# A decoder trunk on one core: the feed-forward input's sums, splits and products in another order

## The chip, the cores and the metric

One Trainium2 chip, of which the kernel uses one core. The time is the device time of one execution in microseconds (us). Three runs of the kernel before took 1914.89, 1920.9 and 1922.11 us, so its median is 1920.9 us. One further execution was taken with the hardware profiler; all durations below come from that one.

## The reference

Two layers; each is a feed-forward block, a mixing block and another feed-forward block. All matrices are float32, the sequence has 512 positions, the width is 1024, and the inner width of the feed-forward is 2816. The change is inside the feed-forward:

```python
def swiglu(x, w_in, w_out):
    gate, up = jnp.split(x @ w_in, 2, axis=-1)
    return (jax.nn.silu(gate) * up) @ w_out

for l in range(DEPTH):
    hn = rms_norm(h, g_ffn1[l]) * (1.0 + sc1) + sh1
    h = h + 0.5 * (1.0 + gt1) * swiglu(hn, w_ffn1_in[l], w_ffn1_out[l])
    ...   # the mixing block
    hn = rms_norm(h, g_ffn2[l]) * (1.0 + sc3) + sh3
    h = h + 0.5 * (1.0 + gt3) * swiglu(hn, w_ffn2_in[l], w_ffn2_out[l])
```

So a feed-forward takes the normed rows `hn`, multiplies them by a gate matrix and an up matrix, and sends silu(gate) times up through an output matrix. Four such blocks run one after the other.

## The kernel before, in words

**Precision.** TensorE multiplies in a shortened float32, so every operand is split in two: ScalarE (ACT) casts it to a high half, and VectorE (DVE) subtracts to get the low half. In the profile these are the line 101 CAST (`wH`, `comH`) and the line 102 TENSOR_TENSOR (`wL`, `comL`). One product then takes three matmuls: high by high, high by low, low by high. Split weights live in four buffers for `wH` and four for `wL`, which rotate.

**The input of a feed-forward.** The 22 blocks of 128 inner columns are 11 pairs, in two groups (pairs 0 to 5 and 6 to 10); after each group its part of the output matrix is multiplied. The first pairs of a block (four in the very first feed-forward, two in the three others) are multiplied directly, in `projector` (line 98). All later pairs, 34 over the whole kernel, go through `pair_in`, which saves one of eight sub-products by a scheme of sums: seven products of 24 matmuls (line 441 to 443) instead of eight. For the gate and up weights a11, a12, a21, a22 of one pair and the halves B of `hn`, it needs combined rows of `hn` (`P1`, `P2`, `T3`, `T4`, made once per feed-forward by `whole` and `combine`) and combined weights:

1. `S` = row sum of a21 and a22, times P1, into bank `ps_f`; ACT copies the result out (`up`, line 459);
2. the first product, a11 times B11, into bank `ps_d`; ACT copies it out (`s1`, line 463);
3. the last product (a22 times T4) of the *pair before*, which was left waiting (`flush`); the first pair of a group has nothing waiting here;
4. the second weight sum, `S` plus a11 (line 464), times P2, added on top of `ps_d`; ACT copies it out (`s2`, line 468);
5. the corner product, a12 times B21, into bank `ps_g`; DVE adds `s1` (`gate`, line 472) and ACT applies silu;
6. the third sum times T3, added on top of `ps_d`;
7. the sum `S` plus a12 (line 474), times B22, into `ps_f`.

Products 2, 4 and 6 share one bank: each may start only when the copy of what was there before has been read out.

**What sets the order.** A list scheduler writes out one fixed order for each engine from the order of the program text, its own cost estimates and the free buffers. On the chip every engine works through its own list strictly in order and waits at an instruction until what it needs is there. The loads of the weights are issued from SP's queue, the adding loads (which sum two weight blocks while loading) from POOL's queue, each in order too. `issue_after(x)` makes what is written inside it stand behind instruction x on x's own engine.

Of the kernel before, what the change touches and what calls it, by code (L numbers as in the profile page):

```python
# [11 lines left out]
AF = mybir.ActivationFunctionType  # L12
ALU = mybir.AluOpType
# [44 lines left out]
def trunk_kernel(ctx, tc, ins, out, layers=L, phases=("ffn1", "mix", "ffn2")):  # L58
    nc = tc.nc
# [11 lines left out]
    tt, stt, ts = nc.vector.tensor_tensor, nc.vector.scalar_tensor_tensor, nc.vector.tensor_scalar  # L71
    act, mm = nc.scalar.activation, nc.tensor.matmul

    def E(name="e", dt=F32):
        return sp.tile([P, T], dt, name=name, tag="e", bufs=4)
# [4 lines left out]
    def psum(shape, name, tag="x"):  # L80
        return ps.tile(shape, F32, name=name, tag=tag, bufs=2)
# [18 lines left out]
    def split(hi, lo, src):  # L100
        nc.scalar.copy(hi, src)  # L101
        nc.vector.tensor_sub(lo, src, hi.bitcast(F32))  # L102
# [261 lines left out]
    def ffn(l, w_in, w_pair, w_out, hn, im, ss, need, then, ready, first=None):  # L364
# [6 lines left out]
        with tc.tile_pool(name="act", bufs=1) as ap_:  # L371
            com = {n: tuple(ap_.tile([P, 4, H2], F32R, name=x, tag="com", bufs=8) for x in ("comH", "comL")) for n in ("P1", "P2", "T3", "T4")}
            ap_.tile([P, (512 - GAP) // 4], F32, name="gap", tag="gap")
            n_first = 2 if first is None else 4
            tiles = (t for t in projector([w_in[l, j, g] for j in range(2 * n_first) for g in range(2)], hn, BANKS[:3], first, 1, ready) if t is not None)
            xs, waiting, done, after = {}, [], [None], [None]

            def flush():
                for f in waiting:
                    done[0] = f()  # L380
                waiting.clear()

            def hl(w):
                pair = tuple(wp.tile([P, KD, P], F32R, name=x, tag=x, bufs=4) for x in ("wH", "wL"))
                split(*pair, w)
                return pair

            def raw(src, tag=None):
                w = (ap_.tile if tag else wp.tile)([P, KD, P], F32, name=tag or "wraw", tag=tag or "wraw", bufs=1 if tag else 2)
                with tc.issue_after(after[0].ins) if after[0] else nullcontext():  # L390
                    nc.sync.dma_start(w, src)
                return w

            def plus(w, src):
                nc.gpsimd.dma_start(w, src, accum_op=ALU.add)

            def new_x(p):

                X = tuple(ap_.tile([P, 2, T], F32R, name=x, tag="act", bufs=12) for x in ("actH", "actL"))
                for i in range(2):  # L400
                    xs[2 * p + i] = tuple(x[:, i] for x in X)
                return X
# [30 lines left out]
            P1, P2, T3, T4 = ([tuple(t[:, k] for t in com[n]) for k in range(4)] for n in ("P1", "P2", "T3", "T4"))  # L433
            B11, B21, B22 = ([tuple(t[:, sl] for t in hn[k0 + k]) for k in range(4)] for k0, sl in ((0, lo_), (4, lo_), (4, hi_)))

            def prod(pt, w, x, start):

                for i in range(2):
                    for k in range(4):
                        wH, wL = (t[:, 4 * i + k] for t in w)  # L440
                        mm(pt[:, i], wH, x[k][0], start=start and i + k == 0, stop=False, skip_group_check=True)  # L441
                        mm(pt[:, i], wH, x[k][1], start=False, stop=False, skip_group_check=True)  # L442
                        mm(pt[:, i], wL, x[k][0], start=False, stop=k == 3, skip_group_check=True)  # L443

            def put(X, sl, x):
                nc.scalar.copy(X[0][:, :, sl], x)
                return tt(X[1][:, :, sl], x, X[0][:, :, sl].bitcast(F32), ALU.subtract)

            def pair_in(p):
                A = lambda g, kh: w_pair[l, p, g, kh]  # L450
                turns = ("r0", "r1") if p % 2 else ("r1", "r0")
                pD, pF, pG = (psum([P, 2, H2], n, t) for n, t in zip(("ps_d", "ps_f", "ps_g"), ("mm",) + turns))
                X = new_x(p)
                half_ = lambda n: E(n).rearrange("p (i t) -> p i t", i=2)
                S = raw(A(1, 0), ("sum0", "sum1")[p % 2])
                plus(S, A(1, 1))
                prod(pF, hl(S), P1, True)
                up = half_("up")
                nc.scalar.copy(up, pF)
                a11 = raw(A(0, 0), "first")  # L460
                prod(pD, hl(a11), B11, True)
                s1 = half_("s1")
                nc.scalar.copy(s1, pD)  # L463
                tt(S, S, a11, ALU.add)
                flush()
                prod(pD, hl(S), P2, False)
                s2 = half_("s2")
                nc.scalar.copy(s2, pD)  # L468
                a12 = raw(A(0, 1))
                prod(pG, hl(a12), B21, True)  # L470
                gate = half_("gate")
                tt(gate, pG, s1, ALU.add)
                act(gate, gate, AF.Silu)
                tt(S, S, a12, ALU.add)
                S3 = raw(A(0, 0), "third")
                plus(S3, A(1, 0))
                prod(pD, hl(S3), T3, False)
                tt(up, pD, up, ALU.add)
                prod(pF, hl(S), B22, False)
                tt(s2, pF, s2, ALU.add)  # L480
                act(s2, s2, AF.Silu)
                tt(up, s2, up, ALU.mult)
                put(X, hi_, up)

                def rest():
                    prod(pD, hl(raw(A(1, 1))), T4, False)
                    tt(gate, pD, gate, ALU.mult)
                    return put(X, lo_, gate)

                waiting.append(rest)  # L490
# [8 lines left out]
                    yield k0, n, load_w(w_out[l, i, :, k0 : k0 + n], n, w)  # L499


            when = {8 * (n_first == 4) + m: n for m, n in ((1, 0), (3, 1), (4, "P1"), (5, "P2"), (6, "T3"), (7, "T4"))}
            beside = lambda m: m in when and (combine if type(when[m]) is str else whole)(when[m])
            crep = ada_crep(ap_) if n_first == 4 else None
            for g, (j0, j1) in enumerate(GROUPS):
                for p in range(j0 // 2, j1 // 2):
                    if p < n_first:
                        X = new_x(p)
                        for j in (2 * p, 2 * p + 1):
                            pg = next(tiles)  # L510
                            beside(2 * j)
                            pu = next(tiles)
                            s = E("silu")
                            act(s, pg, AF.Silu)
                            stt(s, s, -1.0, pu, ALU.mult, ALU.mult)
                            nc.scalar.copy(xs[j][0], s)
                            behind = tt(xs[j][1], s, xs[j][0].bitcast(F32), ALU.subtract)
                            beside(2 * j + 1)
                            if n_first == 4:
                                ada_steps(ap_, crep, (0, 0, 4, 4, 0, 3, 0, 0)[j], behind)  # L520
                    else:
                        after[0] = None if g or p > n_first + 1 else loads[-2]
                        pair_in(p)
                        after[0] = None
# [26 lines left out]
            n = (j1 - j0) // 2  # L551
# [693 lines left out]
    for n, (l, p) in enumerate(seq):  # L1245
        im = what[p][1]
        nss = new_ss() if n + 1 < len(seq) else None
        nxt, ws = [], []

        def then():  # L1250
            if nss is None:
                return [lambda *_: None] * 5
            nhn, scale, *steps = normed(n + 1, nss)
            nxt.append(nhn)
            scale()
            l2, p2 = seq[n + 1]
            if p2 == "mix":
                srcs = [ins["wmi"][l2, k] for k in range(4)]
            else:
                srcs = [ins["w1i" if p2 == "ffn1" else "w2i"][l2, *divmod(k, 2)] for k in range(4)]  # L1260
            return steps + [lambda k, raw: ws.append(load_w(srcs[k], KD, raw))]

        if p == "mix":
            with tc.tile_pool(name="mix", bufs=1) as mp:
                marks = mix(l, hn, nss, mp, then, ready)
        else:
            w, need = ("w1", (l, 7)) if p == "ffn1" else ("w2", (l + 1, 1))
            marks = ffn(l, ins[w + "i"], ins[w + "p"], ins[w + "o"], hn, im, nss, need, then, ready, first)
        first = None
        hn, ready = (nxt[0], (ws, marks)) if nxt else (None, None)  # L1270
# [85 lines left out]
```

## Time and profile before

| what | value |
|---|---|
| median of three runs | 1920.9 us |
| the profiled execution's own time | 1922.28 us |
| its span, first to last instruction | 1920.5 us |
| TensorE (PE) busy | 1884.7 us, 98% |
| DVE busy | 1400.5 us, 73% |
| ACT busy | 838.1 us, 44% |
| `pair_in` calls | 34, of which 8 are the first of a group |
| matmuls of one pair | 7 x 24 = 168 |

The rows of the timeline read: start in us, length in us, engine, line, operation, output<-input, shapes, count, and in brackets the idle time of that engine just before, with what ended it. A matmul's length in the rows (0.28 us) is modelled and overlaps the next one; from start to start two matmuls of 256 columns are 0.11 us apart. PEld is the load of a matmul's weights. In a view of windows, each row is one stretch of time with the busy time and number of matmuls in it and the granted clock of TensorE (1.00 is full).

### The profile page before, as it was taken

To read this page: it belongs to the slowest core of one execution; us is meant where nothing else is said; L and a number is where in the kernel's file an instruction comes from. 1 tells how busy PE (TensorE), PEld (TensorE's weight loads), DVE (VectorE), ACT (ScalarE), POOL (GpSimd) and SP (SyncE) were. 2 spreads that over 40 slices of the span, in tenths; PEclk is the share of its full clock that TensorE was granted. 3 is DMA by queue.
4 is the path that set the end of the run, shared out by engine and by line. 5 is a ranking of instruction groups with operands and counts; after the bars stand their busy time and mean duration, and the time that the engine had idled before them with its cause. 6 is when DMAs were issued, how large, how long until landed. Compare 5 with 4: busy or idle time off the path is not lost. (4 is left out here: it accounts for less than half of the span.)

```text
span 1920.5 us, 37038 instructions
## 1 busy us (share of the span) xinstructions
PE 1884.7 (98%) x15504; PEld 1747.4 (91%) x15504; DVE 1400.5 (73%) x2181; ACT 838.1 (44%) x1264; POOL 130.9 (7%) x212
## 2 busy tenths in 40 slices
PE   8999999999999999999999999999999999999999
PEld 7998899997889999899899989989878899988998
DVE  7687687758976777777867777876598677773862
ACT  4443355356322554155345514544552234532551
POOL 0101100000000001100100020010000000110000
PEclk9999999999999999999999999999999999999999
DMA  7767877421322476877726688781212306765741
GB/s 299 250 165 227 264 194 237 156 69 46 79 60 62 122 198 178 296 201 197 258 73 182 169 264 236 199 278 41 88 54 50 98 23 184 183 212 136 197 139 59
DMA packets 104326, 308.46 MB, mean 161 GB/s; under 512 B 23392, under 2 KB 24416, under 8 KB 103136
## 3 DMA queue, kind: packets, MB, share of 16 engines
q1 hardware_dynamic: 75936, 203.33, 32.2%
q0 software_dynamic: 28224, 102.77, 21.4%
q8 instruction: 121, 1.98, 0.4%
q14 instruction: 45, 0.37, 0.1%
HBM read 302.66 MB, written 3.41 MB: 159 GB/s over the span
## 5 line engine op out<-in xcount | busy, mean ns | idle before, releaser
L101 ACT CAST wH<-wraw 128x1024 fp32r<-128x1024 f32 (+2 forms) x292 | 268.3, 922 | 511.7 <-PE ps_mm L91 175.2
L102 DVE TENSOR_TENSOR wL<-wraw,wH 128x1024 fp32r<-128x1024 f32 (+2 forms) x292 | 308.2, 1059 | 106.7 <-ACT wH L101 105.1
L90 PE MATMUL ps_mm<-actH,wH 128*128 128x512 f32 (+1 forms) x784 | 288.5, 368 | 0.0
L91 PE MATMUL ps_mm<-actL,wH 128*128 128x512 f32 (+1 forms) x784 | 288.0, 367 | 0.0
L92 PE MATMUL ps_mm<-actH,wL 128*128 128x512 f32 (+1 forms) x784 | 288.0, 367 | 0.0
L441 PE MATMUL ps_d<-comH,wH 128*128 128x256 f32 x816 | 228.9, 280 | 4.4 <-ACT s L463 3.6
L443 PE MATMUL ps_d<-comH,wL 128*128 128x256 f32 x816 | 227.3, 279 | 0.0
L442 PE MATMUL ps_d<-comL,wH 128*128 128x256 f32 x816 | 227.3, 279 | 0.0
L98 PE MATMUL ps_mm<-hnH,wH 128*128 128x256 f32 x1040 | 213.6, 286 | 5.8 <-ACT hnH L101 2.9
L98 PE MATMUL ps_mm<-hnL,wH 128*128 128x256 f32 x1040 | 211.8, 283 | 0.0
L98 PE MATMUL ps_mm<-hnH,wL 128*128 128x256 f32 x1040 | 209.3, 281 | 0.5 <-DVE wL L102 0.5
L163 DVE SCALAR_TENSOR_TENSOR wada<-wada,crep 128x1024 f32<-128x1024 f32 x140 | 167.9, 1220 | 46.3 <-DMA wada<-in_wadaT 46.0
L102 DVE TENSOR_TENSOR wL<-sum,wH 128x1024 fp32r<-128x1024 f32 x102 | 124.9, 1225 | 75.8 <-ACT wH L101 75.6
L98 PEld LDWEIGHTS ps_mm<-hnH,wH 128*128 128x128 f32 x1040 | 159.3, 189 | 16.7 <-issue 8.2
L101 ACT CAST wH<-sum 128x1024 fp32r<-128x1024 f32 x102 | 107.5, 1054 | 152.0 <-PE ps_d L442 71.4
L92 PEld LDWEIGHTS ps_mm<-actH,wL 128*128 128x128 f32 x784 | 147.8, 188 | 24.4
L90 PEld LDWEIGHTS ps_mm<-actH,wH 128*128 128x128 f32 x784 | 147.8, 189 | 24.2
L91 PEld LDWEIGHTS ps_mm<-actL,wH 128*128 128x128 f32 x784 | 147.8, 189 | 24.2
L98 PEld LDWEIGHTS ps_mm<-hnL,wH 128*128 128x128 f32 x1040 | 160.0, 189 | 6.7 <-issue 5.7
L98 PEld LDWEIGHTS ps_mm<-hnH,wL 128*128 128x128 f32 x1040 | 159.8, 190 | 4.0 <-issue 2.9
L441 PEld LDWEIGHTS ps_d<-comH,wH 128*128 128x128 f32 x816 | 155.2, 190 | 6.9 <-ACT s L463 5.1
L442 PEld LDWEIGHTS ps_d<-comL,wH 128*128 128x128 f32 x816 | 155.3, 190 | 0.0
(402 smaller groups left out, 4245.5 us busy)
## 6 DMA issues: line engine op xcount, KB each, us to landing
wada<-in_wadaT POOLq DMA_DIRECT2D x128, 512.0 KB, 4.9
wraw<-in_wmi SPq DMA_DIRECT2D x40, 512.0 KB
wraw<-in_w2p SPq DMA_DIRECT2D x36, 512.0 KB
wraw<-in_w1p SPq DMA_DIRECT2D x32, 512.0 KB
wraw<-in_w1o SPq DMA_DIRECT2D x32, 384.0 KB
wraw<-in_w2o SPq DMA_DIRECT2D x32, 384.0 KB
wraw<-in_w1i SPq DMA_DIRECT2D x20, 512.0 KB
wraw<-in_w1o SPq DMA_DIRECT2D x32, 320.0 KB
```

The source lines that it names most:

```text
L90: mm(acc, wH, xH, start=start, stop=False)
L91: mm(acc, wH, xL, start=False, stop=False)
L92: mm(acc, wL, xH, start=False, stop=stop)
L98: mm(acc[:, sl], w[a][:, k], x[b][:, sl], start=start and n == 0 and sl is HALVES[0], stop=stop and n == 2, skip_group_check=True)
L101: nc.scalar.copy(hi, src)
L102: nc.vector.tensor_sub(lo, src, hi.bitcast(F32))
L163: stt(w, w, 1.0, crep, ALU.mult, ALU.mult, accum_out=out_)
L441: mm(pt[:, i], wH, x[k][0], start=start and i + k == 0, stop=False, skip_group_check=True)
L442: mm(pt[:, i], wH, x[k][1], start=False, stop=False, skip_group_check=True)
L443: mm(pt[:, i], wL, x[k][0], start=False, stop=k == 3, skip_group_check=True)
```

## The change

```diff
--- before
+++ after
@@ pair_in @@
                 a11 = raw(A(0, 0), "first")
                 prod(pD, hl(a11), B11, True)
                 s1 = half_("s1")
-                nc.scalar.copy(s1, pD)
+                copied = nc.scalar.copy(s1, pD)
                 tt(S, S, a11, ALU.add)
+
+                def corner():
+                    a12 = raw(A(0, 1))
+                    prod(pG, hl(a12), B21, True)
+                    gate = half_("gate")
+                    tt(gate, pG, s1, ALU.add)
+                    act(gate, gate, AF.Silu)
+                    return a12, gate
+
+                early = None if waiting else corner()
                 flush()
-                prod(pD, hl(S), P2, False)
+                with tc.issue_after(copied.ins):
+                    second = hl(S)
+                prod(pD, second, P2, False)
                 s2 = half_("s2")
                 nc.scalar.copy(s2, pD)
-                a12 = raw(A(0, 1))
-                prod(pG, hl(a12), B21, True)
-                gate = half_("gate")
-                tt(gate, pG, s1, ALU.add)
-                act(gate, gate, AF.Silu)
+                a12, gate = early or corner()
                 tt(S, S, a12, ALU.add)
                 S3 = raw(A(0, 0), "third")
                 plus(S3, A(1, 0))
@@ ffn @@
-            when = {8 * (n_first == 4) + m: n for m, n in ((1, 0), (3, 1), (4, "P1"), (5, "P2"), (6, "T3"), (7, "T4"))}
+            turns_ = (9, 11, 12, 13, 14, 15) if n_first == 4 else (0, 1, 2, 3, 4, 5)
+            when = dict(zip(turns_, (0, 1, "P1", "P2", "T3", "T4")))
             beside = lambda m: m in when and (combine if type(when[m]) is str else whole)(when[m])
```

Three edits. The cast of the second weight sum to its high half stands behind the copy of the first product on ACT, in all 34 pairs. In the first pair of a group the corner product is written before the second one, so in the place that the waiting product of the pair before has in other pairs. In the three feed-forwards with two direct pairs the row sums and combined rows are written at places 0 to 5 of the direct pairs instead of 1, 3, 4, 5, 6, 7; the first feed-forward keeps its places. Nothing is added to the computation or taken from it.

What the scheduler makes of it shows at three places. First ACT in the first `pair_in` of the second feed-forward. Names: `sum_7803` is S of that pair and `sum_8003` that of the next, `wraw` is a12, `third` the third sum; the first row with `sum_7803` splits S plus a11, the second one S plus a12; `s_7866` is s1, and s2 is `s_7897` before and `s_7930` in the change. Before:

```order
L101 CAST wH<-sum_7803 128x1024
L101 CAST wH<-wraw 128x1024
L516 CAST actH<-silu 128x512
L101 CAST wH<-third 128x1024
L459 COPY up<-ps_f 128x512
L101 CAST wH<-sum_7803 128x1024
L463 COPY s_7866<-ps_d 128x512
L101 CAST wH<-sum_8003 128x1024
L468 COPY s_7897<-ps_d 128x512
```

and in the change (lines behind 463 are 8 or more higher):

```order
L101 CAST wH<-wraw 128x1024
L523 ACTIVATE silu<-ps_mm 128x512
L525 CAST actH<-silu 128x512
L459 COPY up<-ps_f 128x512
L463 COPY s_7866<-ps_d 128x512
L101 CAST wH<-sum_7803 128x1024
L101 CAST wH<-third 128x1024
L471 ACTIVATE gate<-gate 128x512
L101 CAST wH<-sum_7803 128x1024
L480 COPY s_7930<-ps_d 128x512
```

Before, the cast of S plus a12 stood ahead of the copy s1; now both casts of S stand behind s1, and the cast of S plus a12 stands ahead of the copy s2. On DVE, same pair, before:

```order
L464 TENSOR_TENSOR sum_7803<-sum_7803,first 128x1024
L515 SCALAR_TENSOR_TENSOR silu<-silu,ps_mm 128x512
L102 TENSOR_TENSOR wL<-sum_7803,wH 128x1024
L102 TENSOR_TENSOR wL<-wraw,wH 128x1024
L517 TENSOR_TENSOR actL<-silu,actH 128x512
L474 TENSOR_TENSOR sum_7803<-sum_7803,wraw 128x1024
L102 TENSOR_TENSOR wL<-third,wH 128x1024
```

and in the change:

```order
L464 TENSOR_TENSOR sum_7803<-sum_7803,first 128x1024
L102 TENSOR_TENSOR wL<-wraw,wH 128x1024
L524 SCALAR_TENSOR_TENSOR silu<-silu,ps_mm 128x512
L526 TENSOR_TENSOR actL<-silu,actH 128x512
L102 TENSOR_TENSOR wL<-sum_7803,wH 128x1024
L102 TENSOR_TENSOR wL<-third,wH 128x1024
L470 TENSOR_TENSOR gate<-ps_g,s_7866 128x512
L482 TENSOR_TENSOR sum_7803<-sum_7803,wraw 128x1024
L102 TENSOR_TENSOR wL<-sum_7803,wH 128x1024
```

The split of a12 moved up, right behind S plus a11; S plus a12 moved down, behind the split of the third sum and the addition of the corner product.

The second place is PE in the same pair, from the end of the second product (`ps_d<-comH`) to the third; waits are shown. Before, the rest of the corner product stood there:

```order
L443 MATMUL ps_d<-comH,wL 128x256
L442 MATMUL ps_g<-hnL,wH 128x256
L443 MATMUL ps_g<-hnH,wL 128x256
...
L441 MATMUL ps_f<-hnH,wH 128x256
L442 MATMUL ps_f<-hnL,wH 128x256
L441 MATMUL ps_d<-comH,wH 128x256 [waits Activation_49]
```

and in the change:

```order
L443 MATMUL ps_d<-comH,wL 128x256
L441 MATMUL ps_f<-hnH,wH 128x256 [waits Activation_49]
L442 MATMUL ps_f<-hnL,wH 128x256
L441 MATMUL ps_d<-comH,wH 128x256 [waits Activation_49]
```

Before, 11 of the corner's 24 matmuls lay between the second and the third product (13 lay between the first and the second), then two of the last product, `ps_f`. Now all 24 lie between the first and the second, and behind the second only the two of `ps_f` are left, with a wait for ACT of their own.

The third place is ACT in a pair that is not the first of its group, here the second pair of the second feed-forward (`sum_8003` its S, `wraw` its a12, `gate` the gate half of the pair before). Before:

```order
L101 CAST wH<-sum_8003 128x1024
L481 ACTIVATE s_7897<-s_7897 128x512
L101 CAST wH<-wraw 128x1024
L446 CAST actH<-up 128x2x256
L459 COPY up<-ps_f 128x512
L101 CAST wH<-third 128x1024
L463 COPY s_8066<-ps_d 128x512
```

and in the change:

```order
L446 CAST actH<-up 128x2x256
L459 COPY up<-ps_f 128x512
L463 COPY s_8066<-ps_d 128x512
L101 CAST wH<-sum_8003 128x1024
L101 CAST wH<-wraw 128x1024
L101 CAST wH<-third 128x1024
L446 CAST actH<-gate 128x2x256
```

The cast of the second sum moved from five places ahead of the copy s1 to right behind it, and the casts of a12 and of the third sum moved behind it too.

## The prediction, made before the changed kernel ran

> **What bounds the kernel now.** I read the page's busy line first, then the waits of PE, then windows around the places named there.
>
> ```profile
> PE 1884.7 (98%) x15504; PEld 1747.4 (91%) x15504; DVE 1400.5 (73%) x2181; ACT 838.1 (44%) x1264; POOL 130.9 (7%) x212
> ```
>
> PE has work for 98% of the span. No other engine can become the bound on average; a change of order can only take away moments in which PE waits, or make new ones. Whom it waits for (in total, times, longest):
>
> ```profile
> PE ps_g L443 <- DVE wL L102: 4.5, 3, 2.6
> PE ps_d L441 <- ACT s L463: 3.6, 2, 1.8
> ```
>
> The corner product waited three times for its low weights, the second product twice for the copy s1. What such a place costs in all shows in windows that run from the end of the first product (a11) of the first pair of a group to the start of the next pair: 4 x 24 matmuls each. The last row is one pair later in a group, all 168 matmuls (the counts take in those that overlap an edge).
>
> ```profile
> 127.38:139.01 11.63, 11.45 (x99) 1.00 0.71 188
> 231.70:243.31 11.61, 11.45 (x98) 1.00 0.83 212
> 826.10:837.72 11.62, 11.46 (x99) 1.00 0.77 184
> 1173.03:1184.82 11.79, 11.66 (x99) 1.00 0.71 185
> 1770.67:1782.28 11.61, 11.45 (x98) 1.00 0.83 183
> 678.77:695.13 16.36, 13.62 (x99) 0.90 0.81 202
> 1026.47:1042.17 15.70, 13.02 (x98) 0.89 0.83 204
> 1622.60:1639.82 17.22, 14.48 (x98) 0.80 0.79 195
> 262.39:281.47 19.08, 19.08 (x170) 1.00 0.73 195
> ```
>
> A later pair has no gap at all: 19.08 / 168 x 96 = 10.90 us would do for 96 matmuls. Five of the eight first pairs lose 0.73, 0.71, 0.72, 0.89 and 0.71, together 3.8 us. The three at 679, 1026 and 1623 us, the first pairs of the feed-forwards with two direct pairs, lose 5.46, 4.80 and 6.32, together 16.6 us. So 20.4 us hang on the eight first pairs, and nothing on the 26 others. That is the most the change can win.
>
> Part of it is the clock: the granted clock fell to half for single windows of 3.41 us behind a window in which PE was idle for long. Four windows of that grid: the first brought the second to half clock; the last two brought none:
>
> ```profile
> 681.26:684.67 3.41, 1.62 (x14) 1.00 0.95 205
> 684.67:688.08 3.41, 3.41 (x18) 0.50 0.99 364
> 677.85:681.26 3.41, 2.47 (x21) 1.00 0.69 160
> 585.68:589.09 3.41, 2.30 (x21) 1.00 0.28 85
> ```
>
> Busy 1.62 of 3.41 us brought a half-clock window; busy 2.47 did not (the row before it), nor 2.30 elsewhere. A half-clock window costs 3.41 / 2 = 1.7 us.
>
> **What the change removes.** At 679 us:
>
> ```profile
> 675.41 1.22 DVE L464 TENSOR_TENSOR sum<-sum,first 128x1024 f32<-128x1024 f32 x1
> 678.94 1.22 DVE L102 TENSOR_TENSOR wL<-wraw,wH 128x1024 fp32r<-128x1024 f32 x1
> 680.68 1.22 DVE L474 TENSOR_TENSOR sum<-sum,wraw 128x1024 f32<-128x1024 f32 x1
> 681.98 1.04 ACT L101 CAST wH<-sum 128x1024 fp32r<-128x1024 f32 x1 [1.32 <-DVE sum L474]
> 682.93 0.58 ACT L463 COPY s<-ps_d 128x512 f32<-128x512 f32 x1
> 683.57 0.38 PE L441 MATMUL ps_d<-comH,wH 128*128 128x256 f32 x1 [1.79 <-ACT s L463]
> ```
>
> The split of a12 (678.94) ends 1.2 us after PE wanted it, and the copy s1, free to run since about 679, sits on ACT behind a cast that waits for the sum S plus a12. In the new order neither happens: the split of a12 follows the sum of line 464, and nothing stands ahead of s1. Also four row sums and two half combinations, 6 x 0.6 = 3.6 us, go into a hole of DVE ahead of the busy stretch (two row sums into an earlier one), so all that follows comes earlier:
>
> ```profile
> 643.67 0.48 DVE L256 SCALAR_TENSOR_TENSOR hnL<-hn_t,mod,hnH 128x256 fp32r<-128x256 f32 x1 [0.18 <-ACT hnH L250]
> 647.10 1.23 DVE L102 TENSOR_TENSOR wL<-wraw,wH 128x1024 fp32r<-128x1024 f32 x1 [2.94 <-ACT wH L101]
> 652.18 1.29 DVE L411 TENSOR_TENSOR x<-hnH,hnL 128x512 f32<-128x512 f32 x2
> ```
>
> I cost the moved sums at nothing: the hole of 2.94 us takes them; without it the split at 647.10 would slip by up to 3.6 - 2.9 = 0.7 us, and the product behind it has not waited there. So all present losses of the eight first pairs go: -20.4 us.
>
> **What it adds: the second product of every pair.** Count from T, the first matmul after the a11 product. DVE read a finished bank 0.20 us after the next product's start (259.67 and 259.87 below); I take the same for ACT. Then: copy s1 at T+0.20; the cast behind it 0.48 later (688.96 to 689.44), 1.05 long, to T+1.73; the split 0.04 later, 1.23 long (268.00 + 1.05 to 269.09), to T+3.00; PE sees it 0.05 later (678.94 + 1.22 to 680.21), T+3.05.
>
> ```profile
> 259.67 0.28 PE L441 MATMUL ps_f<-hnH,wH 128*128 128x256 f32 x1
> 259.87 0.69 DVE L478 TENSOR_TENSOR up<-ps_d,up 128x512 f32<-128x512 f32 x1 [0.25 <-PE ps_d L443]
> 688.96 0.58 ACT L468 COPY s<-ps_d 128x512 f32<-128x512 f32 x1
> 689.44 1.05 ACT L101 CAST wH<-first 128x1024 fp32r<-128x1024 f32 x1
> 268.00 1.05 ACT L101 CAST wH<-third 128x1024 fp32r<-128x1024 f32 x1 [0.71 <-ACT up L459]
> 268.96 0.58 ACT L463 COPY s<-ps_d 128x512 f32<-128x512 f32 x1
> 269.09 1.23 DVE L102 TENSOR_TENSOR wL<-third,wH 128x1024 fp32r<-128x1024 f32 x1 [0.82 <-ACT wH L101]
> 678.88 0.19 PEld L442 LDWEIGHTS ps_g<-hnL,wH 128*128 128x128 f32 x1
> 680.21 0.19 PEld L443 LDWEIGHTS ps_g<-hnH,wL 128*128 128x128 f32 x1 [1.15 <-DVE wL L102]
> ```
>
> 24 matmuls lie between (2.72 us), and the low weights are first used by the third matmul, whose load would start one matmul early, at T+2.72+0.23-0.11 = T+2.84. PE loses 0.2 us, in each of 34 pairs. Bounds: 0 (the load only has to precede its own matmul at T+2.95, and ACT answers 0.1 sooner) and 0.4; I take 0.2, from the nearest rows. In the 26 later pairs: +5.2 us. The later casts of such a pair have room: the copy s2 would end by the same kind of count about T+7.5, and the third product comes at T+8.4.
>
> **What it adds: the third product of a group's first pair.** Here the corner no longer covers the copy s2, and ACT's list has the cast of S plus a12 ahead of s2, that sum stands late in DVE's list, and PE's two `ps_f` matmuls need that cast. The chain from T, by steps from start to start: split of S at T+1.77; split of the third sum 1.14 later, T+2.91; corner's addition 1.14 later, T+4.05; S plus a12 0.60 later, T+4.65, 1.22 long (as L474), to T+5.87; its cast 0.05 later, T+5.92, to T+6.97; s2 0.95 after its start (268.00 to 268.96), T+6.87, to T+7.45; PE 0.06 later (682.93 + 0.58 to 683.57), T+7.51, and 0.1 for a load that could not run ahead: T+7.61. PE's own work until then is 24 + 24 + 2 matmuls, 5.67 us. Loss 1.94 us, the 0.2 above included; at eight places +15.5 us. Bounds: 1.3 (waits shorter by a step of 0.6) and 2.4 (the cast of the third sum late). The same head-of-line wait that held s1 at 682.93 now holds s2, in all eight groups rather than in two.
>
> **Loads.** The buffers of a12 and of the third sum come free 5 to 7 us later in every pair. Third sum: in a group's first pair its load was issued at 217.96 and the cast could start at 229.56.
>
> ```profile
> 217.96 0.33 SPq L391 DMA_DIRECT2D third<-in_w1p  x1
> 229.56 1.05 ACT L101 CAST wH<-third 128x1024 fp32r<-128x1024 f32 x1 [2.39 <-DMA third<-in_w1p]
> ```
>
> 11.6 us; now issued at about T+7.6 it lands at T+19.2, and the next pair casts it at T+21.9. I cost this at nothing, with 2.7 us to spare; beyond it, each us late is one us of PE in 26 pairs.
>
> **Sum:** -20.4 + 15.5 + 5.2 = +0.3 us, on 1922.28 of the profiled execution 1922.6, and 1.4 less for the median: about 1921 us. The stall is moved, not removed.
>
> [...]
>
> **The rivals.** *The change does what its words say (faster).* The chain to s2 is shorter than counted or hidden, and first pairs lose only the 0.2. Then -20.4 + 34 x 0.2 = -13.6: 1907 us. For it: both causes of the waits at 679 are gone in the lists. Against: both waits stand in PE's list, and every step of the chain is a row. Chance 0.14.
>
> *Half clock behind the new stalls (slower).* Place: the window around the third product of each first pair. With 1.25 us idle PE is busy about 2.1 of 3.41 us, between 1.62 (half clock) and 2.30 (not), and nearer the latter; the grid must also hold the stall whole. If all eight fell, +8 x 1.7 = 13.6: 1935 us; it is slower by over 0.5% from six on. Chance 0.12.
>
> *The old stalls stay (the change does not do what it says).* DVE is still late at 679, 1026 and 1623, for a load or a cast earlier in the list. Then the 16.6 - 3 x 1.94 = 10.8 us remain beside the new costs: 1932 us. Against: in the new list the split of a12 depends on nothing late. Chance 0.07.
>
> **How the numbers follow.** Forecast: 1921 us, chance 0.67, with its own range 1912 (no loss in the second product, the chain 0.5 shorter) to 1931 (0.4 in each pair, 2.4 in a first one). With the rivals, 1908 to 1934 leaves out about 2 in 10. Half a per cent, 9.6 us, is about what can be told from no change here. Faster by more: the first rival almost whole and a little of the forecast's low end, 0.15; slower by more: most of the second and third and a little of the high end, 0.20; between 0.65.
>
> **What would show it.** Right: PE waits in the changed profile are gone from `ps_g` and from the first copy, and new are eight waits of about 1.2 us of `ps_f` L441 for ACT's cast; windows as above are 12.8 us long at all eight places; a later pair takes 19.3 instead of 19.08 us; the clock stays full in the feed-forwards. Wrong: first-pair windows near 11.1 us; later pairs at 19.08; half clock behind the third product; or a wait for a DMA of the third sum or a12.

## The result, and the profile after

The changed kernel takes 1936.7 us (median of eight runs, 1931.8 to 1941.5) against 1921.4 us (1914.9 to 1928.3); the ratio is 1.0074, with a 95% interval of 1.0057 to 1.0091. It is slower by 0.74%, some 14 us, and lies outside the forecast's range of 1908 to 1934 us. The forecast of "no change, 1921 us" is wrong.

The profiled execution after took 1936.09 us with a span of 1934.3 us, so 13.8 us more span than before. First the page's busy line:

```profile
PE 1893.3 (98%) x15504; PEld 1748.6 (90%) x15504; DVE 1385.1 (72%) x2181; ACT 837.8 (43%) x1264; POOL 130.8 (7%) x212
```

The matmuls are the same 15504, yet PE is "busy" 8.6 us longer (1893.3 against 1884.7). So most of the loss will not be found as idle time. Next the waits of PE:

```profile
PE ps_f L441 <- ACT wH L101: 9.6, 8, 1.2
PE ps_mm L92 <- DVE wL L102: 3.4, 3, 2.1
PE ps_d L443 <- DVE wL L102: 0.3, 1, 0.3
```

The old waits of `ps_g` and of the first copy s1 at 679, 1026 and 1623 us are gone, and the eight new waits of 1.2 us before the third product are there, as forecast. Not forecast: three waits in the output products (line 92). And the wait of the second product for its low weights, forecast in all pairs, seems to be there once. Windows over the same stretches as before (from the end of the a11 product to the next pair's start), two of the first pairs, and then three later pairs from start to start:

```profile
128.38:141.30 12.92, 11.70 (x99) 1.00 0.64 156
686.11:698.92 12.81, 11.65 (x98) 1.00 0.50 132
248.18:267.54 19.36, 19.36 (x170) 1.00 0.69 187
267.54:287.30 19.76, 19.76 (x170) 1.00 0.73 190
287.30:307.20 19.90, 19.90 (x171) 1.00 0.70 182
```

First pairs take 12.8 to 12.9 us at seven places and 13.1 at one, with the clock full. The forecast said 12.8: gains at three places, losses at five. Over the eight pairs, start to start, the two profiles differ by -4.8 us; the forecast's two terms, -20.4 and +15.5, give -4.9. The whole loss is therefore elsewhere: in the 26 later pairs with the output products behind them. Before, such a pair took 19.08 us (two of them 19.20 and 19.21), now 19.36 to 19.90 us. The pairs are busy for all of it. The stall shows only from start to start of single matmuls; here PE in the second product of the pair at 248, with what ACT and DVE did for it (the first row is the first matmul behind the a11 product, the T of the prediction):

```profile
253.66 0.28 PE L441 MATMUL ps_d<-comH,wH 128*128 128x256 f32 x1
253.92 0.59 ACT L463 COPY s<-ps_d 128x512 f32<-128x512 f32 x1 [1.76 <-PE ps_d L443]
254.40 1.05 ACT L101 CAST wH<-sum 128x1024 fp32r<-128x1024 f32 x1
255.49 1.23 DVE L102 TENSOR_TENSOR wL<-sum,wH 128x1024 fp32r<-128x1024 f32 x1 [3.09 <-ACT wH L101]
256.50 0.28 PE L442 MATMUL ps_d<-comL,wH 128*128 128x256 f32 x1
256.77 0.39 PE L443 MATMUL ps_d<-comH,wL 128*128 128x256 f32 x1
256.99 0.28 PE L441 MATMUL ps_d<-comH,wH 128*128 128x256 f32 x1
```

From 256.50 to 256.77 are 0.27 us instead of 0.11, and to the next 0.22. The copy, cast and split stand in a chain, as forecast, and the split ends at 256.72. But a matmul's length in the profile (0.28 us) is longer than its distance to the next (0.11), so the end of 256.50 is drawn at 256.78 and no idle time is left to be listed. This wait of 0.27 us is counted as busy time. A window's length over the same matmuls shows it; a list of waits does not.

### The profile page after: what moved, and what is told of

It reads as the page before. It is cut to its first block, busy times and chain, and to the rows that moved or that the text cites. A ratio compares the mean times of both kernels' runs of the same rounds, so it can differ in the third digit from the quotient of the medians.

```text
span 1934.3 us, 36973 instructions
## 1 busy us (share of the span) xinstructions
PE 1893.3 (98%) x15504; PEld 1748.6 (90%) x15504; DVE 1385.1 (72%) x2181; ACT 837.8 (43%) x1264; POOL 130.8 (7%) x212
## 3 DMA queue, kind: packets, MB, share of 16 engines
HBM read 302.66 MB, written 3.41 MB: 158 GB/s over the span
## 5 line engine op out<-in xcount | busy, mean ns | idle before, releaser
L443 PEld LDWEIGHTS ps_d<-comH,wL 128*128 128x128 f32 x816 | 153.1, 188 | 6.4 <-DVE wL L102 5.4
```

## The experiments

The kernel before ran beside every group of runs: its medians there were 1918.9 us (first four kernels), 1923.05 us (next four) and 1921.48 us (last two). The ratios are against these. Theory A: the loss is all due to the first edit, the second sum's split behind the copy s1, in the later pairs. Theory B: it is due to loads and queues that all three edits push later.

### One edit taken out, or one alone

`no_split`: the change with the second sum's split free again.

```diff
-                with tc.issue_after(copied.ins):
-                    second = hl(S)
-                prod(pD, second, P2, False)
+                prod(pD, hl(S), P2, False)
```

> The change without its first edit (the second weight sum's split is free again to go ahead of the copy s1; sums at earlier places and corner second stay). In its order PE has 24 corner matmuls between first and second product and 13 of the last product between second and third in a group's first pair. Theory A (the loss sits in the split behind s1: 0.27 us of waiting in the second product of every pair, a slower pace of PE behind some of these waits, 0.118 instead of 0.113 us a matmul, and the chain to s2 in first pairs): later pairs take 19.08 us again, first-pair windows 10.9 to 11.6 us, no waits at the low weights of the second product; 1902 to 1908 us. Theory B (the loss comes from loads and splits that are issued later because buffers come free later and from queues behind them): those come from the corner's and the sums' new places too, the time stays at 1925 us or above.

Measured: 1906.4 us, ratio 0.9935 (0.9917 to 0.9953). Faster than both kernels. Windows of a first pair and of a later pair:

```profile
679.39:690.62 11.23, 11.15 (x98) 1.00 0.89 225
243.55:262.63 19.08, 19.08 (x170) 1.00 0.73 188
```

All first pairs but one (11.98) are at 11.23 to 11.25 us, the later ones at 19.08 (one 19.21), and nothing waits at the output products. Start to start the eight first pairs are 17.1 us under the kernel before, where the change has 4.8, so the first edit costs 12.3 us in them beside what it costs in the later pairs. Taking out one edit of three turns +0.74% into -0.65%. That is theory A.

`split_alone`: only that edit, in the kernel before.

```diff
-                prod(pD, hl(S), P2, False)
+                with tc.issue_after(copied.ins):
+                    second = hl(S)
+                prod(pD, second, P2, False)
```

> The first edit alone: the split of the second weight sum stands behind the copy s1, everything else as before. In its order a first pair has only two matmuls (of the corner) behind the first two of the second product. Theory A: later pairs 19.36 us and some 19.8 to 19.9 (as in the change), first pairs about 13.5 us in the windows, since cast and split behind s1 are bare there: 3 x -2.9 and 5 x +1.9 against before, about 0 together; 26 x 0.27 = 7, slower pace about 4, waits at the output products about 3: 1935 us. Theory B: without the other two edits the loads keep their times, later pairs show the 0.27 but nothing beside it: 1929 us or less.

Measured: 1953.5 us, ratio 1.0187 (1.0162 to 1.0212): much worse than either theory said. Waits, and the windows of two first pairs from start to start (before: 21.84 and 17.39 us) with a granted clock below full:

```profile
PE ps_d L441 <- ACT wH L101: 13.3, 9, 1.7
PE ps_g L441 <- ACT wH L101: 3.6, 8, 0.4
681.92:703.53 21.61, 18.91 (x146) 0.92 0.71 184
1185.88:1208.29 22.41, 19.29 (x146) 0.92 0.64 167
```

Later pairs took 19.36 to 19.92 us as Theory A said. What it missed is half clock: in first pairs the bare chain behind s1 left PE idle, and in five of the eight a window with PE busy 1.35 to 1.59 of 3.41 us was followed by one at a clock of 0.50 (below, under the hardware). Without the corner product in front of it the first edit costs the first pairs +12.0 us over before, not 0.

`sums_alone` and `corner_alone`: the third and the second edit alone.

```diff
-            when = {8 * (n_first == 4) + m: n for m, n in ((1, 0), (3, 1), (4, "P1"), (5, "P2"), (6, "T3"), (7, "T4"))}
+            turns_ = (9, 11, 12, 13, 14, 15) if n_first == 4 else (0, 1, 2, 3, 4, 5)
+            when = dict(zip(turns_, (0, 1, "P1", "P2", "T3", "T4")))
```

> The third edit alone: row sums and combined rows at places 0 to 5 in three feed-forwards, everything else as before. Theory A: later pairs 19.08; DVE reaches the split of a12 about 3 us earlier in the first pairs at 679, 1026 and 1623 us, the corner's wait of 2.6 us there goes, and with it most of the 16.6 us: 1905 to 1910 us. Theory B: the split of a12 still stands behind S plus a12 and the activations in DVE's list, the waits stay with smaller sizes: 1915 to 1921 us.

```diff
-                flush()
+                early = None if waiting else corner()
+                flush()
                 prod(pD, hl(S), P2, False)
...
+                a12, gate = early or corner()
```

(`corner` is the function of the change.)

> The second edit alone: the corner product second in a group's first pair; sums and splits in their old places. In its order DVE splits a12 directly behind S plus a11, and the copy s1 still stands behind the cast of S plus a12. Theory A: later pairs 19.08; the corner's wait for its low weights goes at all eight places, s1 is still late by about 2.4 us at the three places at 679, 1026 and 1623 us, whose windows become about 13.5 us; the five others 11.2: 10 us under the kernel before, a ratio near 0.995. Rival (without the earlier sums DVE stays too late for any order): the three windows stay at 15 to 17 us, a ratio of 0.999.

Measured: 1909.3 us, ratio 0.9944 (0.9930 to 0.9958), for the sums; 1912.9 us, ratio 0.9956 (0.9943 to 0.9968), for the corner. The window at 679 (16.36 us before) in the two:

```profile
678.65:690.35 11.70, 11.59 (x98) 1.00 0.82 202
...
678.17:691.62 13.45, 11.61 (x99) 1.00 0.82 207
```

Of the 16.6 us of the three places the sums take back 14.2 and the corner 9.0, from start to start; together (`no_split`) it is 15.9, because it is one loss that two edits cure. The corner alone leaves 13.45 us there, since s1 still stands behind the cast of S plus a12, as expected; the rival of `sums_alone` (waits stay) fell.

### Where the first edit costs: first pairs, later pairs, last pairs

`split_first_only` ties the split behind s1 only in first pairs; `split_not_last` ties it in all pairs but the last of each group.

```diff
-                with tc.issue_after(copied.ins):
+                if early:
+                    with tc.issue_after(copied.ins):
+                        second = hl(S)
+                else:
                     second = hl(S)
```

(in the other one the condition is `p not in (5, 10)`.)

> The whole change, but the split of the second weight sum is tied behind s1 only in the first pair of a group; in the 26 later pairs it is free again. Theory A (the later pairs' split brings the 0.27 us, the slower pace, and, by releasing the raw weights later, the late splits at the output products): later pairs 19.08 us, first pairs as in the change (18.3 to 18.5 from start to start), no wait of PE for low weights at the output products: about 4.8 us under the kernel before, a ratio near 0.9975. Rival (the output products are late because of the sums' and the corner's new places): waits of 0.5 to 2 us at the output products stay, a ratio of 1.000 or more.

> The whole change, but in the last pair of each group (the one ahead of an output product) the split of the second weight sum is free again. Theory A (the lateness at the output products enters with the last pair's late splits, whose raw buffers the next loads need): no waits of PE for low weights at the output products, last pairs with their output product as in the kernel before, other later pairs 19.36 to 19.9: -4.8 + 8 = 3 us over the kernel before, a ratio near 1.0015. Rival (it piles up over the later pairs of a group): the waits at the output products stay, a ratio of 1.005.

Measured: 1920.0 us, ratio 0.9994 (0.9980 to 1.0007), and 1927.9 us, ratio 1.0031 (1.0016 to 1.0047). In the first one's profile the first pairs are again 4.8 us under before, later pairs take 19.08 us but for two (19.20 and 21.04), and the span is 5.1 us shorter. The pair of 21.04, at 1184 us, waited for its copy s2, which stood on ACT behind a cast of the next pair's `S`; the adding load of that sum was issued at 1188.88 and landed at 1197.57, and ACT started the cast at 1197.65, after 4.03 us of idle time:

```profile
PE ps_d L441 <- ACT s L483: 1.7, 1, 1.7
```

So the span's -5.1 is near the first pairs' -4.8 in part by luck: the 2.0 us lost in that pair came back in the mixing block from 1243 us on, which took 2.4 us less than before. The runs of this kernel show less on average than expected (0.9994 for 0.9975), and whether it gains at all is open. Against the change it gains 0.8%, about 15 us: that is what the first edit costs in the 26 later pairs. The forecast had 5.2 us for them.

The second one shows where half of this sits (1.0074 - 1.0031, 8 us). The rows: the last pair of the first group with its output product, before, in the change and in `split_not_last` (ahead of the same output), and then a middle pair of the latter:

```profile
1080.33:1167.42 87.09, 87.09 (x482) 1.00 0.73 240
...
1087.06:1178.38 91.32, 89.27 (x483) 0.98 0.73 238
...
1083.37:1170.46 87.09, 87.09 (x482) 1.00 0.77 247
264.95:284.71 19.76, 19.76 (x170) 1.00 0.73 190
```

With the last pair's split free, the output products no longer wait, but for one wait of 0.2 us at 365 us, while the middle pairs keep their 19.36 to 19.88. So the lateness there comes in with the last pair. Eight last pairs at 0.28, two of them at the slower pace, and 5.1 us of waits and half clock at the output products, all of it priced below, are about the 8 us. What is late can be followed at 140 us: the split of a22, which ends the use of its raw buffer, and the second load of modulation weights on POOL's queue, which waits for a split to release its buffer (before, then the change; PE itself is 2.3 us later there):

```profile
151.10 1.23 DVE L102 TENSOR_TENSOR wL<-wraw,wH 128x1024 fp32r<-128x1024 f32 x1 [0.89 <-ACT wH L101]
147.23 0.54 POOL L177 DMA_DIRECT2D wada<-in_wadaT  x1 [8.86 <-DVE wL L102]
...
155.48 1.22 DVE L102 TENSOR_TENSOR wL<-wraw,wH 128x1024 fp32r<-128x1024 f32 x1
154.99 0.55 POOL L177 DMA_DIRECT2D wada<-in_wadaT  x1 [12.89 <-DVE wL L102]
```

4.4 and 7.8 us later. Behind the products of these weights stand the splits of the output weights in DVE's list; at 1170 in the change:

```profile
1170.79 1.23 DVE L163 SCALAR_TENSOR_TENSOR wada<-wada,crep 128x1024 f32<-128x1024 f32 x1
1172.01 0.95 DVE L102 TENSOR_TENSOR wL<-wraw,wH 128x768 fp32r<-128x768 f32 x1
1173.02 0.50 PE L92 MATMUL ps_mm<-actH,wL 128*128 128x512 f32 x1 [2.05 <-DVE wL L102]
```

The split of the output weights ends when PE has waited 2.05 us. That the last pair's split brings these waits is shown; the path through the modulation loads is read from the rows and was not tried by itself.

### The stall of 0.27 us, and what follows it

`lows_later`: the whole change, but in the second product the first four low-weight matmuls come two blocks later. ACT's and DVE's orders are those of the change.

```diff
-            def prod(pt, w, x, start):
+            def prod(pt, w, x, start, late=0):
...
+                    d = late * (1 - i)
...
+                        if k >= d: mm(pt[:, i], w[1][:, j - d], x[k - d][0], start=False, stop=k - d == 3, skip_group_check=True)
...
-                prod(pD, second, P2, False)
+                prod(pD, second, P2, False, 2)
```

> The whole change, with one thing more: in the second product the matmuls with the low weights come two blocks later (the first of them is the seventh matmul, not the third); orders of ACT and DVE are those of the change, word for word. Theory A (the slower pace of PE is left behind by the wait of 0.27 us): without the wait later pairs take 19.08 us and no pair of the feed-forwards has the pace of 0.118; 26 x 0.27 = 7 and 8 x 0.53 = 4 us less than the change: about 1925 us. Rival (the pace comes from the traffic of ACT, DVE and loads at their new places): the 0.27 goes and the slower pace stays in about 8 pairs: about 1930 us.

Measured: 1930.2 us, ratio 1.0048 (1.0031 to 1.0065). In its windows the later pairs take the old time, as here:

```profile
247.75:266.83 19.08, 19.08 (x171) 1.00 0.67 190
```

So without the wait the pairs cost nothing extra, though ACT, DVE and the loads work in the changed order: in these runs the slower pace of the pairs at 19.76 and 19.90 us came with the stall (its rival fell). The one exception fits: in the last pair at 1683 us a matmul of the second product still came 0.09 us late, and the slower pace followed it. The whole gained only 5 us of the 11.7 expected, since the output products were now later still; behind the longest wait, with PE busy 0.80 of 3.41 us from 945.52, the granted clock was 0.68 in the window from 948.93 to 952.34:

```profile
PE ps_mm L92 <- DVE wL L102: 4.9, 4, 2.9
```

What was taken from one wait went partly into the next.

`lows_not_last`: both remedies on the change at once.

> Both remedies together on the change: low weights two blocks later in the second product, and the split free again in the last pair of each group. Theory A in full (waits of 0.27 us, the pace behind them and the late output products are all that the later pairs cost): later pairs 19.08 us, no waits at the output products, only the first pairs' -4.8 is left: about 5 us under the kernel before, a ratio of 0.9975. If something else is in the change's cost, the ratio stays above 1.000.

Measured: 1920.7 us, ratio 0.9998 (0.9986 to 1.0010). In the profile all named costs are gone (a later pair, and a last pair with its output product):

```profile
245.63:264.71 19.08, 19.08 (x170) 1.00 0.66 192
140.08:227.17 87.09, 87.09 (x482) 1.00 0.78 250
```

That takes back 14.6 us of the change's loss (0.0076 of 1921), as `split_first_only` does by another way. The 5 us under the kernel before are again not there on average, though the first pairs of the profile have their -4.8. Of these, 1.5 us went into one late copy s1 at 1681 us, which ACT started after a cast that waited for a load:

```profile
1680.97 1.05 ACT L101 CAST wH<-third 128x1024 fp32r<-128x1024 f32 x1 [3.07 <-DMA third<-in_w2p]
1681.92 0.58 ACT L463 COPY s<-ps_d 128x512 f32<-128x512 f32 x1
```

This is the load of the third sum that the forecast had costed at nothing "with 2.7 us to spare". In the profile another 1.8 us lie behind the last pairs of three feed-forwards, in the output products and mixing blocks. That is within what one kernel shows: from the pair at 1254.82 to the next layer's first `pair_in` at 1629.08 the change took 374.3 us in its first profile and 377.7 (1252.22 to 1629.89) in its second. Why the runs of this kernel and of `split_first_only` show no gain on average stays open.

### The first pairs' new wait

`s2_first`: in first pairs the cast of S plus a12 stands behind the copy s2.

```diff
-                nc.scalar.copy(s2, pD)
+                copied2 = nc.scalar.copy(s2, pD)
...
-                prod(pF, hl(S), B22, False)
+                with tc.issue_after(copied2.ins) if early else nullcontext():
+                    last = hl(S)
+                prod(pF, last, B22, False)
```

> The whole change with one thing more: in a group's first pair the cast of S plus a12 stands behind the copy s2 on ACT, not ahead of it; PE then has the third product directly behind the second one and the whole last product behind the third. Theory A (the cast ahead of s2 costs what the forecast's chain says): the wait of 1.2 us becomes 0.8, the bare copy with its 0.2 ahead, and the two matmuls ahead of the third product no longer wait: first pairs 17.6 us instead of 18.3 to 18.5, 8 x 0.8 = 6 us under the change, a ratio near 1.004 against the kernel before. Rival (the third product waits for the split of its own sum, which is as late): first pairs stay at 18.2 or more, a ratio of 1.007.

Measured: 1930.9 us, ratio 1.0060 (1.0039 to 1.0081); against the change the two intervals overlap, so this is read from the profile:

```profile
PE ps_d L441 <- ACT s L480: 5.6, 8, 0.7
677.85:695.44 17.59, 16.86 (x146) 1.00 0.54 137
```

The eight waits of 1.2 us became eight of 0.7, and seven of the eight first pairs take 17.6 to 17.7 us (18.3 to 18.9 in the change). The cast ahead of s2 was the cost that the chain gave.

### The slower pace in a second execution

> The change itself, profiled a second time, for one question: which of the stalls in the second product leave PE at the slower pace. In the first profile 8 later pairs went slow (behind 276, 296, 911, 1656, 1676, 1695, 1821 and 1841 us) though all had the same wait of 0.27 us or, once, 0.55. Theory C (it is a matter of a few ns of phase between PE and DVE at the moment of the restart): other pairs go slow this time, about as many. Rival (something at these places, a load or a neighbour on ACT or DVE, decides): the same eight.

Measured: 1935.7 us. This time five later pairs ran slow behind the stall, at 869, 1074, 1656, 1696 and 1822 us; three of these are among the eight of the first profile, and the one at 1696 had a wait of 0.55 us both times. The rows: the pair at 266 which was slow at first and not now, and the pair at 860, the other way round (19.36 in the first profile):

```profile
265.80:285.16 19.36, 19.36 (x171) 1.00 0.70 190
860.41:880.17 19.76, 19.76 (x171) 1.00 0.73 189
```

It is not bound to the place, with at most that one exception. The first pairs together are only 3.2 us under the kernel before in this profile (4.8 in the first one); the one at 1174 us took 19.85 us, and PE was busy 0.91 of the 1.71 us from 1177.62 in it.

## Why the prediction was wrong

**Right.** What the change removes: the old losses of the first pairs went whole. The chain to s2: eight waits of 1.2 us for the cast, windows of 12.8 us, full clock behind them. First pairs together -4.8 us for -4.9.

**Wrong: "PE loses 0.2 us ... in the 26 later pairs: +5.2 us".** The mechanism was right, the size was not. In the rows above T is 253.66. The copy started 0.25 us after T in 25 of the 26 pairs (the rounded rows show 0.26), not 0.20; the 0.20 was DVE's, and the prediction took the same for ACT. The steps behind it were as forecast, so the split ended at T+3.05 instead of T+3.00, and PE went on at T+3.10 instead of T+3.05. The prediction's 3.05 - 2.84 = 0.21 thus became about 0.26, and the first matmuls behind the restart brought it to 0.28. The later pairs cost about 17 us in the profile, made of four parts:

| part | forecast | measured |
|---|---|---|
| the wait itself, 26 times | 0.2 each, 5.2 | 19.36 - 19.08 = 0.28 each, 7.3 |
| the slower pace behind it | not seen | 8 stretches of 125 matmuls (below), 125 x (14.72/125 - 19.08/168) = 0.52 each, 4.2 |
| waits at the output products | 0 | 0.8 + 0.6 + 2.05 = 3.4 |
| half clock behind the longest of these | 0 | one window at a clock of 0.50, 3.41 / 2 = 1.7 |

The sum is 16.6 for 5.2, and with the first pairs' -4.8 it is +11.8 of the 13.8 us; 1.0 of the rest lies ahead of the first `pair_in`, where nothing was changed. With the wait alone the sum would still have been near nothing (7.3 - 4.8 = 2.5); the three parts that were left out, 9.3 us, are what turned "no change" into slower.

**Wrong: "Loads ... I cost this at nothing".** The step went through the a12 and third-sum loads inside a group, with their 2.7 us to spare, and not to the group's end. There the late split of the last pair made the output products wait (`split_not_last`). By the rows, a raw buffer came free 4.4 us later at 140 us and a load of modulation weights was issued 7.8 us later, and the products of these weights stand ahead of the output weights' splits; that path was not tried by itself. The step should have followed a later release through every user of the same buffers.

**The rivals.** "The change does what its words say", 1907 us, is what the change without its first edit does (1906.4 us), by other terms: first pairs -17.1 us, and nothing lost in the second products. "Half clock behind the new stalls", 1935 us, came near the measured time by another way: none of the eight fell; the lowest busy time of a window there was 2.19 of 3.41 us, and the clock stayed at 1.00. "The old stalls stay" fell.

**The range** let the second product cost at most 0.4 in each pair. The slow pairs lost 0.7 to 0.8 (19.76 and 19.90), and nothing in it allowed for the output products.

**Two readings of the profile before.** Half clock came in single windows at 684 and 1029 us, but at 1626.75 us in two in a row; and two of the 26 later pairs lost 0.12 and 0.13 us. Neither moves the sum.

## What to carry to other kernels

When an edit moves work behind another instruction in every turn of a loop, price its smallest lateness by the number of turns, and follow the buffers that it releases later to their next users, also past the loop's end. A fix meant for the first turn should stand in the first turn alone; better here was not to make it, since earlier sums and the corner product had already cured the wait (0.65% faster instead of 0.74% slower). And compare window lengths over equal work: the 26 waits of about 0.27 us here lay under the drawn end of a matmul (0.28 us) and were counted as busy time.

## What the hardware showed that was not expected

**Two paces at full clock.** The same products ran at 0.113 or at 0.118 us a matmul while the granted clock was 1.00. Two windows of 14.72 us in the change, one behind a stall that left the fast pace, one behind a stall that left the slow one:

```profile
256.99:271.71 14.72, 14.72 (x131) 1.00 0.63 171
276.13:290.85 14.72, 14.72 (x125) 1.00 0.62 173
```

Behind the stall in the second product the slow pace began in 8 and in 5 of 26 later pairs with about the same stall, and, where a pair came next, ended in that pair's first (a11) product. The same pace stands in the kernel before as well: behind a matmul that came 0.36 us after the one ahead, at 1179.3 us, it held for some 70 matmuls of 0.118 us, to 1187.6 us, which is why the pair at 1184.82 took 19.21 us. In the first profile of the change the matmul after the restart followed it by 0.225 to 0.227 us in the 8 later pairs that went slow and by 0.220 to 0.223 in the 18 that did not; one first pair, at 839.29 us, went slow with 0.224. What decides is not shown.

**Half clock behind windows in which PE was busy for 1.36 and 1.59 of 3.41 us.** Windows of that length in the change, then in `split_alone`, then in `split_first_only`:

```profile
133.15:136.56 3.41, 2.19 (x17) 1.00 0.74 192
1170.80:1174.21 3.41, 1.36 (x6) 1.00 0.75 240
1174.21:1177.62 3.41, 3.41 (x9) 0.50 0.83 229
...
1193.46:1196.88 3.42, 1.59 (x10) 1.00 0.08 32
...
1196.51:1199.92 3.41, 1.74 (x15) 1.00 0.52 204
```

Busy 2.19 and 1.74 us brought none; 1.59 (the window behind it, at 1196.88 us, had a clock of 0.50) and 1.36 were followed by half clock, like the 1.62 before. The busy time alone does not sort them: early in the change's profile, where PE ran other products, windows at a clock of 1.00 with PE busy 1.83 us (17.06 to 20.47) and 2.57 us (27.30 to 30.71) were followed by half clock too. (At half clock already, a window with PE busy 2.76 us, at 1626.75 us in the kernel before, was followed by another one at half clock.)
